# A transformer block in split fp32: w_out requested and cast later in the merge, another order of turns and operands at the entrance of the up stage, shorter norm steps

## The chip, the core and the metric

The kernel runs on one core of a Trainium2 chip. A core has TensorE (PE, matmuls), VectorE (DVE), ScalarE (ACT), GpSimd (POOL) and SyncE (SP), which here issues the DMAs; 16 DMA engines move data between HBM and SBUF. Each engine works through its own row of instructions in order, and semaphores hold an instruction back until what it reads is there. The metric is the time of one execution on the device in microseconds, as a median of runs.

## The reference

One layer of a hybrid block over 1024 tokens of width 1024, all in float32. Cut to the steps that matter here:

```python
attn = banded_window_attention(q, k, v, kc, vc, sink[l])
# merge_branches:
m = sigmoid(g_a) * (attn @ w_pa) + sigmoid(g_f) * (fourier_mix(f) @ w_pf)
y = m @ w_out
x = x + gt1 * rmsnorm(y, g_post1)
h2 = modulate(rmsnorm(x, g_pre2), sh2, sc2)      # h * (1 + scale) + shift
u, gate = split(h2 @ w_up)                       # ConvFFN, d_ff = 2816
u = u[:-2] * conv_w[0] + u[1:-1] * conv_w[1] + u[2:] * conv_w[2] + conv_b
x = x + gt2 * rmsnorm((silu(u) * gate) @ w_down, g_post2)
```

`rmsnorm(x, g)` is `x * rsqrt(mean(x*x) + eps) * g`.

## The kernel before

**Split products.** Every float32 operand of a large product is cast to a shorter type (the "hi" part, on ACT), and the rest, value minus hi, is the "lo" part (on VectorE, `sub`). `mm3` multiplies hi by hi, hi by lo and lo by hi: three matmuls of 128x128 by 128x512 for one step k. So nearly all of TensorE's operands come by an ACT cast and a VectorE subtraction. In the names, `h...` or `...h` is hi and `l...` or `...l` is lo.

**The program is one list.** Nothing is scheduled later: each engine's row has the order in which the Python code calls the steps. A step that is called earlier goes ahead on all engines that it uses.

**Merge.** Sixteen tiles `PA[i]` = (j, h): 128 channels j of m by 512 tokens h. `pa_mm` makes attn @ w_pa for one (12 matmuls, PSUM tile `pa`). `pa_out` multiplies it by the sigmoid gate (`sga`, read back from HBM), adds the Fourier half (`mf`, read back too) and casts `mh`; `pa_low` makes `ml`. `pa_load` requests `sga` and `mf` of the tile three ahead, into a ring of eleven buffers (`so`). `merge(i)` does the matmuls of tile i and then the sums of tile i-1. The first two tiles are made ahead of this loop (EARLY = 2). The w_pa tiles for j = 4 to 7 (`wpa`, parts `whpa` and `wlpa`) and the first half of w_out (`wor`, hi and lo parts in `w0a`, `w0b`) are loaded and cast inside the loop: `merge(i)` requests w_out's k = i - 2, casts it, and on even i does the same for a w_pa tile. w_out's second half (`woh`, `wol`) comes behind the loop.

**y = m @ w_out.** `y_mm(tk, h, ks)` adds steps k to a tile of 128 tokens tk by 512 columns h. `y_token` does the norm of y, the residual and the norm of x (`y_square`, `y_norm`, `y_gate`, `y_res`, `x_sq`, `z_scale`). `y_norm` takes the mean square v, a square root on ACT, a reciprocal r on VectorE, and one Newton step r (1.5 - 0.5 v r r). `y_turn` transposes z on TensorE (eight matmuls against the identity, `ptz`), and `y_affine` applies scale and shift (a2, s2) from PSUM in eight pieces, on VectorE (V) or ACT (None).

**Up stage.** h2 @ w_up in Winograd's form of Strassen's algorithm: the activations give the operands B11, B21, T1, T2, T3, T4n, B22 (`hb_puts` casts and subtracts four column tiles c; `t1` to `t4` are the sums ahead of it on `h`), the weights give P1, P2, P5, P6, P7 (`conv` makes hP on ACT, lP on VectorE). `mm(n)` is one product, accumulated in PSUM as `X_u`, `Y_u`, `Z_u`; `evac(n)` takes it out (`snP`, and `u` sums on VectorE); `ahead(n)` makes weight parts that come next. All three are called from a list written out by hand at the entrance, and from a table behind it.

Of the kernel before, what the change touches and what calls it, by code (L numbers as in the profile page):

```python
# [12 lines left out]
AF = mybir.ActivationFunctionType  # L13
# [22 lines left out]
def fbits(ap):  # L36
    return ap.bitcast(F)
# [26 lines left out]
def block_kernel(ctx: ExitStack, tc: tile.TileContext, t: dict, out: bass.AP, dbg: dict):  # L64
# [18 lines left out]
    def s(name, dtype=F):  # L83
        return spool.tile([P, 512], dtype, tag="s", name=name, bufs=40)
# [1369 lines left out]

    wo, w0s = {}, []

    def wo_load(k, h):
        raw = s(f"wor{k}{h}")
        load(out=raw, in_=t["w_out"][k * P:(k + 1) * P, h * 512:(h + 1) * 512])
        if h == 0:  # L1460
            if k == 0:
                w0 = [hbl.tile([P, 3, 512], R, tag="ha", name=f"w0a{i}", bufs=4) for i in range(4)]
                w0 = [w0[i][:, j, :] for i in range(4) for j in range(3)]
                w0s.extend(w0 + [hbl.tile([P, 1, 512], R, tag="hb", name=f"w0b{i}", bufs=4)[:, 0, :] for i in range(4)])
            wo[k, h] = (w0s[2 * k], w0s[2 * k + 1])
        else:
            wo[k, h] = (o2(f"woh{k}{h}", "w1", 16), o2(f"wol{k}{h}", "w1", 16))
        copy(wo[k, h][0], raw)
        return lambda: sub(wo[k, h][1], raw, fbits(wo[k, h][0]))

    def merge(i):

        j, h = PA[i]
        pa_mm(j, h, ps(f"pa{j}{h}"))
        if i + 3 < len(PA) and PA[i + 3] not in pal:
            pa_load(*PA[i + 3], so)
        low = []
        if i - EARLY < KT:
            low.append(wo_load(i - EARLY, 0))
        if i % 2 == 0 and 4 <= i // 2 + 2 < KT:  # L1480
            raw, m = merge_raw(t["w_pa"], i // 2 + 2, "pa"), i // 2 + 2
            paw[m] = s(f"whpa{m}", R), s(f"wlpa{m}", R)
            copy(paw[m][0], raw)
            low.append(lambda: sub(paw[m][1], raw, fbits(paw[m][0])))
        if i > EARLY:
            pa_out(*PA[i - 1])
        for f in low:
            f()
        if i > EARLY:
            pa_low(*PA[i - 1])  # L1490
# [26 lines left out]
    def y_norm(tk, n, fill=()):  # L1517

        fill = list(fill)

        def between():
            if fill:
                fill.pop(0)()

        ss = ssy[:, tk, 2 * n[0]:2 * n[0] + 2 * len(n)]
        v, sq, r, n1 = (tiny(f"{q}y{tk}{n[0]}", 2, 8)[:, :len(n)] for q in ("v", "sq", "r", "n1"))
        add(v, ss[:, 0::2], ss[:, 1::2])
        nc.vector.tensor_scalar(out=v, in0=v, scalar1=1.0 / D, scalar2=EPS, op0=ALU.mult, op1=ALU.add)
# [310 lines left out]
    with tc.manual_schedule():  # L1839
# [41 lines left out]
        for f in [wo_load(k, 1) for k in range(4, KT)]:
# [251 lines left out]
```

## Time and profile before

| | us |
|---|---|
| median of 3 runs (lowest, highest) | 1311.36 (1310.92, 1312.81) |
| the profiled execution, its own time | 1312.6 |
| its span in the profile | 1310.8 |
| busy in the span: TensorE, VectorE, ACT, GpSimd | 1260.3, 1034.5, 683.3, 231.5 |

The profiled execution is one more execution of the same program; its span is from its first to its last instruction. TensorE is busy for 96% of it, and is 73% of the chain of work that ended last, VectorE 15%. "Busy" counts the time in which an engine executes something, not the time in which it stands waiting. In a row of the trace, `[3.29 <-ACT whpa L1483]` says that the engine stood idle for 3.29 us ahead of this instruction, and that what released it was ACT's instruction on line 1483 that wrote `whpa`. `x4` on a row joins four like instructions that follow each other. The merge lies from about 515 to 563 us of the span, y from 563 to 658, and the up stage begins there.

### The profile page before, as it was taken

The numbers are of one execution on the slowest core, as the hardware profiler recorded it, in microseconds if no ns is written. First come the engines' busy times: TensorE is split into PE (matmuls) and PEld (weight loads), VectorE is DVE, ScalarE is ACT, GpSimd is POOL, SyncE is SP. The second block draws the span as 40 slices with busy tenths as digits, with TensorE's granted clock in tenths as the row PEclk, the third lists the DMA queues.
The fourth block names the chain that finished last, engine by engine and source line by source line (L and its number), as shares of the span: only waits on it lengthen the run. The fifth ranks groups of instructions, "written<-read, shape, count | busy, mean of one in ns | idle before, by whom it ended". The sixth has DMA issues, their size and how long they took to land.

```text
span 1310.8 us, 18510 instructions
## 1 busy us (share of the span) xinstructions
PE 1260.3 (96%) x5998; PEld 1022.7 (78%) x5998; DVE 1034.5 (79%) x1890; ACT 683.3 (52%) x1358; POOL 231.5 (18%) x191
## 2 busy tenths in 40 slices
PE   5999999999999999899999999999999999999996
PEld 3768777888878877778867888888888887888884
DVE  4866768884888996677879998999888877666767
ACT  7754347433667775344566655445444445544442
POOL 0001211100333333000000023535554200000000
PEclk9999999999999999999999999999999999999998
DMA  9997464605233444745213586777867669987884
GB/s 314 352 328 222 143 219 147 192 21 162 59 113 112 127 131 128 267 154 153 89 41 97 148 255 208 225 219 221 250 185 211 196 210 296 370 262 226 285 283 148
DMA packets 271573, 254.56 MB, mean 194 GB/s; under 512 B 16732, under 2 KB 206836, under 8 KB 271476
## 3 DMA queue, kind: packets, MB, share of 16 engines
q1 hardware_dynamic: 271476, 253.38, 61.8%
q8 instruction: 47, 0.77, 0.2%
q14 instruction: 50, 0.41, 0.1%
HBM read 179.65 MB, written 73.40 MB: 193 GB/s over the span
## 4 chain that ended last, share of the span: by engine, by line
PE 73%; DVE 15%; ACT 4%; DMA 3%; issue 3%; SPq 1%; POOL 1%; DVEq 0%; POOLq 0%; ACTq 0%
PE X_u L110 5%; PE X_u L108 5%; PE X_u L109 5%; PE X_d L110 3%; PE X_d L109 3%; PE X_d L108 3%; PE Y_u L108 3%; PE Y_u L110 3%; PE Y_u L109 3%; PE X_g L108 2%; PE X_g L110 2%; PE X_g L109 2%; DVE p L1199 2%; DVE pl L91 2%; PE Y_d L108 1%
## 5 line engine op out<-in xcount | busy, mean ns | idle before, releaser
L91 DVE TENSOR_TENSOR lP_u<-A_u,hP_u 128x512 fp32r<-128x512 f32 x132 | 106.9, 814 | 23.1 <-ACT hP_u L330 21.4
L392 ACT COPY snP_u<-X_u 128x512 f32<-128x512 f32 x57 | 33.4, 586 | 131.8 <-PE X_u L110 131.7
L392 ACT COPY snP_d<-X_d 128x512 f32<-128x512 f32 x48 | 28.2, 587 | 99.0 <-PE X_d L110 94.9
L330 ACT CAST hP_u<-A_u 128x512 fp32r<-128x512 f32 x121 | 74.6, 619 | 0.0
L1219 POOL TENSOR_SCALAR p<-p,sm 128x640 f32<-128x640 f32 (+1 forms) x64 | 48.3, 774 | 91.5 <-PE pp L1224 35.3
L103 ACT CAST ph<-pp 128x512 fp32r<-128x512 f32 x76 | 44.3, 584 | 22.2 <-PE pp L1224 20.9
L91 DVE TENSOR_TENSOR pl<-pp,ph 128x512 fp32r<-128x512 f32 x76 | 51.6, 681 | 2.5 <-ACT ph L103 2.0
L91 DVE TENSOR_TENSOR yd<-yd,snP_d 128x512 f32<-128x512 f32 x36 | 24.8, 690 | 34.4 <-ACT snP_d L392 34.4
L1213 ACT ACTIVATE p<-p,nm 128x640 f32<-128x640 f32 (+1 forms) x64 | 51.4, 802 | 0.7 <-DVE nm L1206 0.7
L1199 DVE CUSTOM_DVE_ANT_0 p<-ss,mask 128x640 f32<-128x640 f32 (+1 forms) x64 | 49.9, 780 | 0.0
L91 POOL TENSOR_TENSOR A_u<-A_u,A_u 128x512 f32<-128x512 f32 x28 | 47.4, 1692 | 13.9 <-DVE lP_u L91 6.9
L1224 PE MATMUL pp<-ident,p 128*128 128x128 f32 x304 | 46.6, 273 | 2.8 <-POOL p L1219 1.5
L1224 PEld LDWEIGHTS pp<-ident,p 128*128 128x128 f32 x304 | 37.2, 140 | 11.7 <-POOL p L1219 2.9
L1634 DVE SCALAR_TENSOR_TENSOR tb<-u,vec,tb 128x1024 f32<-128x1024 f32 x22 | 39.5, 1795 | 2.8 <-ACT tb L1631 2.7
L91 POOL TENSOR_TENSOR S_u<-A_u,A_u 128x512 f32<-128x512 f32 x14 | 24.7, 1763 | 88.6 <-DMA g_d0P<-ghP 81.7
L1195 PE MATMUL ss<-kst,qs 128*128 128x384 f32 (+1 forms) x128 | 36.6, 367 | 1.3 <-DVE mx L1199 0.8
L91 DVE TENSOR_TENSOR lP_g<-A_g,hP_g 128x512 fp32r<-128x512 f32 x48 | 33.3, 701 | 5.3 <-ACT hP_g L103 4.3
L91 POOL TENSOR_TENSOR A_u<-S_u,A_u 128x512 f32<-128x512 f32 x14 | 18.7, 1337 | 104.1 <-DVE lP_u L91 104.1
L91 DVE TENSOR_TENSOR wB<-wB,wB 128x512 f32<-128x512 f32 x44 | 37.1, 842 | 0.0
L1635 DVE SCALAR_TENSOR_TENSOR tb<-u,vec,tb 128x1024 f32<-128x1024 f32 x22 | 35.6, 1617 | 0.9
L1235 PE MATMUL po<-pl,vst 128*128 128x512 f32 x76 | 31.3, 411 | 2.6 <-DVE pl L91 2.0
L320 ACT COPY snP_g<-X_g 128x512 f32<-128x512 f32 x24 | 14.1, 588 | 36.4 <-PE X_g L110 35.6
(886 smaller groups left out, 4365.3 us busy)
## 6 DMA issues: line engine op xcount, KB each, us to landing
A_u<-in_w_up SPq DMA_DIRECT2D x88, 256.0 KB, 4.5
wB<-in_w_down SPq DMA_DIRECT2D x44, 256.0 KB, 4.3
wa<-in_w_mod SPq DMA_DIRECT2D x36, 256.0 KB, 5.3
wt_dT<-wB SPq DMA_DIRECT2D x33, 256.0 KB, 2.5
wdB<-in_w_down SPq DMA_DIRECT2D x33, 256.0 KB, 4.4
wdT<-wt_dT SPq DMA_DIRECT2D x33, 256.0 KB, 3.3
A_g<-in_w_in SPq DMA_DIRECT2D x32, 256.0 KB, 5.0
ws<-in_w_mod SPq DMA_DIRECT2D x30, 256.0 KB, 6.0
```

What stands on the lines that cost most here:

```text
L91: return (eng or nc.vector).tensor_tensor(out=out, in0=a, in1=b, op=op)
L103: copy(hi, src)
L108: nc.tensor.matmul(ps, ah, bh, start=start, stop=False, skip_group_check=True)
L109: nc.tensor.matmul(ps, ah, bl, start=False, stop=False, skip_group_check=True)
L110: nc.tensor.matmul(ps, al, bh, start=False, stop=stop, skip_group_check=True)
L330: copy(st[j]["half", p][0], st[j][STA[p]])
L392: copy(d["s" + p], d["X"])
L1199: nc.vector.tensor_tensor_reduce(out=p_, in0=ssc[:, lo:768], in1=self.mk, op0=ALU.add, op1=ALU.max, scale=1.0, scalar=-3.0e38, accum_out=s ...
L1213: nc.scalar.activation(out=self.pt[g], in_=self.pt[g], func=AF.Exp, scale=SCALE, bias=self.m[:, g:g + 1], accum_out=self.sm[:, g:g + 1])
L1219: nc.gpsimd.tensor_scalar(out=self.pt[g], in0=self.pt[g], scalar1=self.sm[:, g:g + 1], scalar2=1.0, op0=ALU.mult, op1=ALU.mult)
L1224: nc.tensor.transpose(pp[:, g * P:(g + 1) * P], self.pt[g][:, j * P:(j + 1) * P], ident)
L1634: nc.vector.scalar_tensor_tensor(out=tb, in0=u[:, 0:1024], scalar=cw[0], in1=tb, op0=ALU.mult, op1=ALU.add)
```

## The change

**Merge.** w_out's first half is requested three merges later (in merges 5 to 12) and cast two merges after its request (7 to 14). A w_pa tile is requested one pair of merges ahead of its cast, and the cast stands ahead of the other work of its merge. Two tiles of w_out's second half are requested in the last merge, two right behind the last sums, four ahead of the residual's loads; their casts stay behind the last sums.

**w_out stage.** Step k=0 of token 2 goes ahead of k = 6, 7 of tokens 0 and 1. For token 2 all eight steps of the second half stand ahead of the turn of token 1 (six before).

**Norm steps.** For one column, four VectorE operations become two: n1 = (r v) r and r = (n1 - 3) r. This r is -2 times that of before, so G1 (two tiles) and a2 are scaled by -0.5 on ACT, once. For two columns (once) four become three.

**Entrance of the up stage.** `mm(1)` runs whole ahead of the turn of token 6. `conv(1, "P5")` and the four T2 sums come sooner, and the last four affines of token 7 go from ACT to VectorE. `evac(11)` goes ahead of the operand B22.

```diff
+    def wo_raw(k, h):
+        wor[k, h] = s(f"wor{k}{h}")
+        load(out=wor[k, h], in_=t["w_out"][k * P:(k + 1) * P, h * 512:(h + 1) * 512])
...
+    for n_, q_ in enumerate([(k, 0) for k in range(KT)] + [(0, 1), (1, 1)]):
+        WO.setdefault(5 + n_ if n_ < 11 else len(PA) - 1, []).append(q_)
+        if q_[1] == 0:
+            WOS.setdefault(min(n_ + 7, len(PA) - 1), []).append(q_)
...
         pa_mm(j, h, ps(f"pa{j}{h}"))
-        if i + 3 < len(PA) and PA[i + 3] not in pal:
-            pa_load(*PA[i + 3], so)
         low = []
-        if i - EARLY < KT:
-            low.append(wo_load(i - EARLY, 0))
         if i % 2 == 0 and 4 <= i // 2 + 2 < KT:
-            raw, m = merge_raw(t["w_pa"], i // 2 + 2, "pa"), i // 2 + 2
+            m = i // 2 + 2
+            raw = wpr.pop(m)
             paw[m] = s(f"whpa{m}", R), s(f"wlpa{m}", R)
             copy(paw[m][0], raw)
             low.append(lambda: sub(paw[m][1], raw, fbits(paw[m][0])))
+        if i % 2 == 0 and 4 <= i // 2 + 3 < KT:
+            m1 = i // 2 + 3
+            wpr[m1] = merge_raw(t["w_pa"], m1, "pa")
+        if i + 3 < len(PA) and PA[i + 3] not in pal:
+            pa_load(*PA[i + 3], so)
+        for q in WO.get(i, ()):
+            wo_raw(*q)
+        for q in WOS.get(i, ()):
+            low.append(wo_load(*q))
...
+    for x in (*G1, a2):
+        nc.scalar.activation(out=x, in_=x, func=AF.Copy, scale=-0.5)
...
-        mul(n1, r, r)
-        mul(n1, n1, v)
-        nc.vector.tensor_scalar(out=n1, in0=n1, scalar1=-0.5, scalar2=1.5, op0=ALU.mult, op1=ALU.add)
-        mul(r, r, n1)
+        if len(n) == 1:
+            nc.vector.scalar_tensor_tensor(out=n1, in0=r, scalar=v, in1=r, op0=ALU.mult, op1=ALU.mult)
+        else:
+            mul(n1, r, r)
+            mul(n1, n1, v)
+        nc.vector.scalar_tensor_tensor(out=r, in0=n1, scalar=-3.0, in1=r, op0=ALU.add, op1=ALU.mult)
...
             y_mm(tk, 0, range(6))
+        y_mm(2, 0, range(1))
...
-            y_mm(tk, 1, range(6))
+            y_mm(tk, 1, range(KT if tk == 2 else 6))
             y_turn(tk - 1)
-            y_mm(tk, 1, range(6, KT))
+            if tk > 2:
+                y_mm(tk, 1, range(6, KT))
...
-        mm(1, range(2))
+        mm(1)
         y_turn(6)
-        mm(1, range(2, 4))
...
         conv(0, "P5")
+        conv(1, "P5")
+        t2(0)
+        t2(1)
         y_affine(6, range(4, 8), None)
-        y_affine(7, range(4, 8), None)
+        y_affine(7, range(4, 8), V)
+        t2(2)
+        t2(3)
         mm(4)
...
         evac(0)
-        conv(1, "P5")
         conv(2, "P5")
         mm(5)
-        for c in range(4):
-            t2(c)
         evac(1)
...
         hb_puts(hb, "T4n", {c: h2[c, 0] for c in range(4)})
+        ahead(11)
+        evac(11)
         hb_puts(hb, "B22", {c: h2[c + 4, 1] for c in range(4)})
-        for k in range(11, 14):
+        for k in range(12, 14):
```

Three places show how the rows move. First ACT at the start of the merge loop, from the last casts of attn (`ah`) on. Before:

```order
L103 CAST ah_5679<-aT_3229 128x512
L103 CAST ah_5683<-aT_3229 128x512
L1468 CAST w0a_5774<-wor_5772 128x512
L1468 CAST w0a_5774<-wor_5801 128x512
L1345 CAST mh_5806<-mf_5668 128x512
L1468 CAST w0a_5775<-wor_5828 128x512
L1483 CAST whpa_5833<-wpa_5831 128x512
L1345 CAST mh_5838<-mf_5672 128x512
L1468 CAST w0a_5776<-wor_5861 128x512
```

After:

```order
L103 CAST ah_5679<-aT_3229 128x512
L103 CAST ah_5683<-aT_3229 128x512
L1345 CAST mh_5796<-mf_5668 128x512
L1518 ACTIVATE G_5703<-G_5703 128x512
L1518 ACTIVATE G_5704<-G_5704 128x512
L1494 CAST whpa_5813<-wpa_5775 128x512
L1345 CAST mh_5824<-mf_5672 128x512
L1345 CAST mh_5850<-mf_5676 128x512
L1494 CAST whpa_5867<-wpa_5816 128x512
L1345 CAST mh_5880<-mf_5688 128x512
L1475 CAST w0a_5904<-wor_5846 128x512
```

The w_out casts (`w0a`) stood first and between the casts of m (`mh`); now three `mh` casts, the two G scales and two w_pa casts (`whpa`) stand ahead of the first of them.

Second, VectorE at the entrance of the up stage, from the first lo part of P5 (`lP_u<-S_u`) on; the rows `h<-h,h` are the T2 sums. Before:

```order
L91 TENSOR_TENSOR lP_u_7262<-S_u_6625,hP_u_7261 128x512
L91 TENSOR_TENSOR lP_u_7299<-S_u_6753,hP_u_7298 128x512
L91 TENSOR_TENSOR lP_u_7303<-S_u_6875,hP_u_7302 128x512
L91 TENSOR_TENSOR h_6402<-h_6820,h_6402 128x512
L91 TENSOR_TENSOR h_6449<-h_6952,h_6449 128x512
L91 TENSOR_TENSOR h_6569<-h_7165,h_6569 128x512
L91 TENSOR_TENSOR h_6697<-h_7221,h_6697 128x512
L91 TENSOR_TENSOR u_7290<-Z_u_7240,snP_u_7296 128x512
L91 TENSOR_TENSOR lP_u_7329<-A_u_6367,hP_u_7328 128x512
```

After:

```order
L91 TENSOR_TENSOR lP_u_7236<-S_u_6612,hP_u_7235 128x512
L91 TENSOR_TENSOR lP_u_7240<-S_u_6736,hP_u_7239 128x512
L91 TENSOR_TENSOR h_6397<-h_6803,h_6397 128x512
L91 TENSOR_TENSOR h_6450<-h_6931,h_6450 128x512
L1594 TENSOR_SCALAR h_7195<-ptz_7189,a_71,s_72 128x128 x4
L91 TENSOR_TENSOR h_6560<-h_7147,h_6560 128x512
L91 TENSOR_TENSOR h_6684<-h_7195,h_6684 128x512
L91 TENSOR_TENSOR lP_u_7281<-S_u_6854,hP_u_7280 128x512
L91 TENSOR_TENSOR u_7272<-Z_u_7214,snP_u_7278 128x512
```

Two T2 sums stand ahead of the third lo part now and two behind four affines that ACT had.

Third, ACT from the last T4n cast on, where `hP_u` and `snP_u` behind the B22 casts belong to `ahead(11)` and `evac(11)`. Before:

```order
L103 CAST T4nb_7099<-h_6697 128x128
L103 CAST B22a_7101<-h_6820 128x3x128
L103 CAST B22a_7101<-h_6952 128x3x128
L103 CAST B22a_7101<-h_7165 128x3x128
L103 CAST B22a_7101<-h_7221 128x3x128
L103 CAST B22b_7103<-h_6820 128x128
L103 CAST B22b_7103<-h_6952 128x128
L103 CAST B22b_7103<-h_7165 128x128
L103 CAST B22b_7103<-h_7221 128x128
L330 CAST hP_u_7543<-A_u_6891 128x512
L320 COPY snP_u_7546<-X_u_7109 128x512
L330 CAST hP_u_7551<-A_u_6511 128x512
```

After:

```order
L103 CAST T4nb_7076<-h_6684 128x128
L330 CAST hP_u_7501<-A_u_6870 128x512
L320 COPY snP_u_7504<-X_u_7086 128x512
L103 CAST B22a_7078<-h_6803 128x3x128
L103 CAST B22a_7078<-h_6931 128x3x128
L103 CAST B22a_7078<-h_7147 128x3x128
L103 CAST B22a_7078<-h_7195 128x3x128
L103 CAST B22b_7080<-h_6803 128x128
L103 CAST B22b_7080<-h_6931 128x128
L103 CAST B22b_7080<-h_7147 128x128
L103 CAST B22b_7080<-h_7195 128x128
L330 CAST hP_u_7525<-A_u_6502 128x512
```

One `hP_u` cast and one `snP_u` copy have moved ahead of the eight B22 casts; the lo part of that cast moves the same way on VectorE.

## Rows read from the trace of the kernel before

**Rows 1.** Stage table: window, busy us per engine (instructions), granted clock, DMA share, GB/s.

```profile
521.00:546.00 25.00, 25.00 (x111) 20.57 (x110) 16.03 (x25) 7.87 (x13) 0.00 (x0) 1.00 0.84 299
546.00:554.00 8.00, 4.71 (x14) 3.42 (x13) 4.77 (x8) 2.89 (x5) 0.00 (x0) 0.79 0.68 203
...
690.00:720.00 30.00, 28.63 (x125) 23.12 (x124) 29.65 (x59) 21.35 (x47) 0.00 (x0) 1.00 0.37 106
```

**Rows 2.** TensorE, merge and w_out: start, duration, engine, line, operation, tiles, idle before.

```profile
546.02 0.39 PE L110 MATMUL pa<-ah,wlpa 128*128 128x512 f32 x1
549.69 0.79 PE L108 MATMUL pa<-ah,whpa 128*128 128x512 f32 x1 [3.29 <-ACT whpa L1483]
...
562.78 0.39 PE L110 MATMUL pa<-ah,wlpa 128*128 128x512 f32 x1
...
586.05 0.39 PE L108 MATMUL y<-w0a,mh 128*128 128x512 f32 x1
```

**Rows 3.** TensorE at the turn of token 1.

```profile
597.65 0.88 PE L185 MATMUL ptz<-ident,z 128*128 128x128 f32 x6 [1.03 <-DVE z L1556]
```

**Rows 4.** TensorE at the entrance of the up stage.

```profile
663.25 0.55 PE L185 MATMUL ptz<-ident,z 128*128 128x128 f32 x3 [1.01 <-ACT z L1554]
...
678.83 0.50 PE L108 MATMUL Y_u<-T1a,hP_u 128*128 128x512 f32 x1 [0.51 <-ACT hP_u L103]
...
686.24 0.50 PE L109 MATMUL X_u<-T2a,hP_u 128*128 128x512 f32 x1 [1.17 <-DVE T2a L91]
...
703.57 0.50 PE L108 MATMUL X_u<-T4na,hP_u 128*128 128x512 f32 x1 [0.94 <-ACT snP_u L320]
...
704.73 0.50 PE L110 MATMUL X_u<-T4na,lP_u 128*128 128x512 f32 x1 [0.43 <-DVE lP_u L91]
```

**Rows 5.** SyncE in the merge: DMA issues.

```profile
523.03 0.33 SPq L1459 DMA_DIRECT2D wor<-in_w_out  x1
...
535.37 0.32 SPq L1329 DMA_DIRECT2D sga<-sga_d  x1
543.00 0.32 SPq L1329 DMA_DIRECT2D mf<-mf_d  x1
```

**Rows 6.** ACT in the merge.

```profile
528.39 0.62 ACT L1468 CAST w0a<-wor 128x512 fp32r<-128x512 f32 x1 [8.79 <-DMA wor<-in_w_out]
...
549.02 0.62 ACT L1483 CAST whpa<-wpa 128x512 fp32r<-128x512 f32 x1 [0.27 <-DMA wpa<-in_w_pa]
```

**Rows 7.** VectorE in the merge: first multiply of four tiles.

```profile
532.59 0.68 DVE L91 TENSOR_TENSOR sga<-pa,sga 128x512 f32<-128x512 f32 x1
...
535.73 0.68 DVE L91 TENSOR_TENSOR sga<-pa,sga 128x512 f32<-128x512 f32 x1
...
558.31 0.68 DVE L91 TENSOR_TENSOR sga<-pa,sga 128x512 f32<-128x512 f32 x1
...
561.01 0.68 DVE L91 TENSOR_TENSOR sga<-pa,sga 128x512 f32<-128x512 f32 x1
```

**Rows 8.** VectorE, two steps of a norm.

```profile
583.30 0.16 DVE L91 TENSOR_TENSOR n1y<-ry 128x1 f32<-128x1 f32 x1
583.50 0.16 DVE L91 TENSOR_TENSOR n1y<-n1y,vy 128x1 f32<-128x1 f32 x1
```

**Rows 9.** Groups by line and form, VectorE: count, busy us, mean ns.

```profile
L173 DVE SCALAR_TENSOR_TENSOR n1d<-rd,vd 128x1 f32<-128x1 f32 x8 | 1.8, 220 | 0.3
```

**Rows 10.** ACT at the entrance of the up stage.

```profile
674.89 2.89 ACT L1568 ACTIVATE h<-ptz,s,a 128x128 f32<-128x128 f32 x8
...
699.96 1.75 ACT L103 CAST B22a<-h 128x384 fp32r<-128x384 f32 x4
```

**Rows 11.** VectorE: four affines of turn 0, then the entrance.

```profile
597.91 1.36 DVE L1570 TENSOR_SCALAR h<-ptz,a,s 128x128 f32<-128x128 f32 x4
...
678.81 1.29 DVE L91 TENSOR_TENSOR lP_u<-S_u,hP_u 128x512 fp32r<-128x512 f32 x2 [3.10 <-ACT hP_u L103]
...
703.99 0.69 DVE L91 TENSOR_TENSOR lP_u<-A_u,hP_u 128x512 fp32r<-128x512 f32 x1
```

More of the change, by code (lines that the diff above doesn't have):

```diff
@@ L1455, in block_kernel @@
     wo, w0s = {}, []
+    wor = {}
+    def wo_raw(k, h):
+        wor[k, h] = s(f"wor{k}{h}")
+        load(out=wor[k, h], in_=t["w_out"][k * P:(k + 1) * P, h * 512:(h + 1) * 512])
     def wo_load(k, h):
-        raw = s(f"wor{k}{h}")
-        load(out=raw, in_=t["w_out"][k * P:(k + 1) * P, h * 512:(h + 1) * 512])
+        if (k, h) not in wor:
+            wo_raw(k, h)
+        raw = wor[k, h]
         if h == 0:
@@ L1469, in wo_load @@
         return lambda: sub(wo[k, h][1], raw, fbits(wo[k, h][0]))
+    wpr = {}
+    WO, WOS = {}, {}
+    for n_, q_ in enumerate([(k, 0) for k in range(KT)] + [(0, 1), (1, 1)]):
+        WO.setdefault(5 + n_ if n_ < 11 else len(PA) - 1, []).append(q_)
+        if q_[1] == 0:
+            WOS.setdefault(min(n_ + 7, len(PA) - 1), []).append(q_)
     def merge(i):
@@ L1871, in block_kernel @@
         pa_out(*PA[-1])
+        wo_raw(2, 1)
+        wo_raw(3, 1)
+        pa_low(*PA[-1])
         low = [wo_load(k, 1) for k in range(4)]
-        for f in (lambda: pa_low(*PA[-1]), *low):
+        for f in low:
             f()
+        for k in range(4, KT):
+            wo_raw(k, 1)
         xr_load(0)
@@ L1894, in block_kernel @@
                 pre(tk - 2, ("A22",))
-            y_mm(tk, 0, range(6))
+            y_mm(tk, 0, range(1 if tk == 2 else 0, 6))
             if tk == 2:
```

## The prediction

> **What bounds the kernel now.** The change touches three stretches: the merge, the w_out stage behind it, and the entrance of the up stage. I read the stage table first, to see whether TensorE is held there, and then TensorE's own rows. From 521 to 546 it is busy 25.00 us of 25 with 111 matmuls, 0.227 us for one, and 12 x 0.227 = 2.72 for a tile of the merge [rows 1]. So a change can win only what TensorE loses standing. Then it stands 3.29 us for a cast of w_pa, and the granted clock falls from 1.00 (the upper level, 2.4 GHz) to a mean of 0.79 from 546 to 554 [rows 1, 2], so part of that stretch is at the lower level of 1.2. From 546.02 to 562.78 lie 48 matmuls, worth 48 x 0.227 = 10.9; they took 16.76. **Lost: 5.9.** The next 96, up to 586.05, took 23.27 for 21.8, from 562.78 on [rows 2]. **Lost: 1.4.** A turn of token 1 waits 1.03 for z [rows 3]. TensorE's rows from 658 to 705 hold five waits: 1.01, 0.51, 1.17, 0.94, 0.43 [rows 4]. **Together 4.1.** All of this sums to 12.4, and each piece is at a place that the change reorders.
>
> **Why the merge is late.** The first w_out tile is requested at 523.03 [rows 5]; its cast begins at 528.39, after ACT has idled for 8.79 [rows 6]: a request takes 5.4 us to land, with the DMA engines 0.84 busy [rows 1]. The cast stands in the merge that requests it, ahead of the casts of m on ACT. VectorE waits with it, and then needs 2.70 us for a tile (558.31 to 561.01) and 3.14 (532.59 to 535.73) where two weight parts fall into it [rows 7]. That is TensorE's own pace, so it never catches up. Its late sums hold the ring of eleven buffers: SyncE issues nothing between 535.37 and 543.00 [rows 5]. The w_pa tile requested behind comes late, and the cast that TensorE waits for begins at 549.02 [rows 6].
>
> **The merge after the change.** The w_pa tile for j=4 takes the place of that first w_out request, so it lands at 523.0 + 5.4 = 528.4. G is requested ahead of it. No row shows a scale of 128x512 in place on ACT; the cast of this shape takes 0.62 [rows 6], and I take that for each of two. With both behind 528.4 at the worst, the cast of w_pa ends at 530.3 and its low part (0.68, as each VectorE step of this shape in [rows 7]) at 530.9. TensorE, not held, starts the tile that reads it at 546.25 - 4 x 2.72 = 535.4: 4.5 us to spare. VectorE by then has the tiles summed that TensorE finished before 525, and goes on from 530.9 with twelve at 2.70 and twice 0.44 more: 530.9 + 32.4 + 0.9 = 564.2. TensorE ends the merge at 546.25 + 4 x 2.72 = 557.1. It then has k 0 to 5 of tokens 0 and 1 and the one step of token 2 that was pulled forward, 13 x 0.68 = 8.8, before it needs k=6 of m at 566; VectorE is past those at about 561. The woh casts follow ACT's last m cast, the first low part of woh can end at 565.4, and TensorE wants it at 557.1 + 17 x 0.68 = 568.7. Both losses go: **-7.3**. With a cycle of 3.0 instead of 2.70 the first low part would be at 569.0, and 0.3 would stay.
>
> **Norm steps.** Four VectorE operations, 0.20 from start to start [rows 8], become two scalar_tensor_tensor. On 128x1 with a pointer as scalar one takes 0.22 elsewhere in this kernel [rows 9]; the one with a constant I put between 0.16 (the small multiply [rows 8]) and 0.22. With 0.04 between them the pair takes 0.44 to 0.5 against 0.8: about 0.3 saved in each of 14 norms, 4.2 us of VectorE, nearly all under TensorE. If the pair took as long as the four, only 0.6 at the turn of token 1 would be lost again. The scales that it needs (two of 128x512, one of 128x8) are some 1.4 us of ACT in idle time, the 8.79 above.
>
> **The turn of token 1.** It waited 1.03 [rows 3]. Both norms of the token are 0.3 shorter, and one k more stands between the token's last matmul and the turn (two moved in front of the turn, one moved out to the start): 0.6 + 0.68 = 1.28. The wait goes with 0.25 to spare: **-1.0**. Turn 0 loses 0.68 of cover and gains 0.6; I allow 0 to 0.2 there, and as much at turn 2.
>
> **The up entrance.** With mm(1) whole ahead of it, turn 6 comes 12 x 0.227 = 2.72 later, and its z was 1.01 late: that wait goes. conv(1, "P5") stood behind eight ACT affines of 2.89 [rows 10]; four now go behind it and four to VectorE, and the 0.51 on hP_u goes. VectorE, idle for 3.10 there [rows 11], starts the T2 sums in that gap. Four affines cost it 1.36 [rows 11], three norms give 0.9 back, so T2's low parts come 3.1 - 0.5 = 2.6 sooner, and TensorE wants them 1.0 + 0.5 sooner: 1.17 + 1.5 - 2.6 leaves 0.1 of that wait. The last two (0.94 on snP_u, 0.43 on lP_u) came behind ACT's casts of B22, the first four of them 1.75 [rows 10], and behind B22's low parts on VectorE, which end where lP_u begins, at 703.99 [rows 11]; hP, snP and lP of evac(11) now come ahead of them. All together **-4.0**, and 0.1 for each of four or five restarts, whose first matmuls take 0.50 instead of 0.39 [rows 2, 4]: **-0.4**.
>
> What comes back: from 690 to 720 VectorE is busy 29.65 of 30 [rows 1]. TensorE gains 4.4 there, VectorE only the 2.6, so what VectorE delivers comes up to 1.8 nearer to its use. What was less ahead becomes a wait; B22's own parts are later by evac(11), about 0.7. I keep 0 to 1.8 and take **+0.3**, near the lower end, as the waits of before come from where things stand in a row and not from VectorE's total.
>
> **A rule that speaks against the change.** At 528.39 a cast of ACT waits for its transfer, and what stands behind it in ACT's row waits too, for 8.79 us [rows 6]. So the G scales ahead of the w_pa cast hand on whatever G is late. Rival 2 prices that from rows. The Trainium skill has it as a rule (TensorE: Matmul & The Clock Gate, "Engine queue depths": ScalarE and VectorE have queues that are strictly first in, first out). The trace agrees with that rule by the same 8.79.
>
> **The sum.** Against the profiled execution of 1312.6 (span 1310.8): -7.3 - 1.0 - 4.0 - 0.4 + 0.3 = -12.4, so 1300.2. The median of the runs, 1311.4, lies 1.2 below that execution: 1311.4 - 12.4 = **1299.0**.
>
> **Rivals.**
> 1. *The entrance gives its gain back.* VectorE is the bound from 690 on, and TensorE only waits elsewhere: 1.8 to 4 of the 4.4 return. For it: 29.65 of 30 busy [rows 1]. Against it: the waits that go were ones of order, three of the five on ACT [rows 4]. Time: 1299.0 + 1.5 to 3.7 = 1300.5 to 1302.7. Chance 0.25.
> 2. *ACT's row hands on a late transfer.* G or w_pa lands later than 5.4 after its request, ACT stands, and the chain on VectorE ends later than 564.2. The slack is 4.5 at the first tile and 3.3 at the start of woh; a wait of 3 to 5 needs a landing of 11 or more. For it: the 8.79 of before [rows 6]; against it: the request itself took 5.4 [rows 5, 6]. Time 1302 to 1304. Chance 0.10.
> 3. *The change does nothing:* VectorE's twelve tiles end the merge, not TensorE. To return 7.3 its chain must end at 575, which takes a cycle of 3.6; the rows have 2.70 and 3.14 [rows 7]. With rival 1 beside it: 1309 to 1313. Chance 0.04.
> 4. *Slower.* A w_out request waits for buffers that VectorE frees, VectorE for a cast, and the cast for the request before. In my walk a turn of that loop is 2.7, and k=7 is requested near 550, lands at 555.4 and is read at 566.6. Were each turn to pay a landing, it would be 2.7 + 5.4 = 8.1. Eight turns use up the 10 us of slack and then the 12.4 of gain from (10 + 12.4) / 8 = 2.8 more a turn, 5.5 in all; at 6.0 the time is 1311.4 + 8 x 0.5 = 1315. For it: the gap at SyncE [rows 5]; against it: requests now run two merges ahead of their casts. Chance 0.03.
>
> **How the numbers follow.** The forecast has 0.58, the rivals 0.25, 0.10, 0.04 and 0.03. The forecast alone spans 1297.8 (nothing comes back, 0.3, and each restart costs 0.2 to 0.3 and not 0.1, 0.9 more) to 1300.5 (all of the 1.8 comes back). Up to 1304 it takes in the first two rivals; down to 1296.3 the 1.5 by which single runs of before lie apart from their median. Under 2 in 10 is left out. About 0.2% (2.6 us) is what a measurement of this kernel can tell from no change; the forecast and rivals 1 and 2 all lie beyond it. Faster 0.93, same 0.04, slower 0.03.
>
> **What would show it.** Right: between 515 and 590 no wait of TensorE over 0.5, the clock at 1.00 all through the merge, the first w_out matmul near 557 instead of 563; no wait at turns 1 and 6, none on snP_u behind T4n. Wrong: a gap of several us at SyncE in the merge; ACT idle on G; TensorE waiting on VectorE for 1 us or more at T3, T4n or B22, or new waits on VectorE from 720 to 800 that sum to over 1.8.

## The result and the profile after

The changed kernel takes 1300.34 us (median of 5 runs, 1299.59 to 1301.67), the kernel before 1312.59 (5 runs, 1310.92 to 1312.97). The ratio is 0.9909, with a 95% interval of 0.9897 to 0.9922: 12.2 us less, where 12.4 less were forecast. The profiled execution took 1300.34, with a span of 1298.6.

The stage table of the changed kernel, with the columns of [rows 1]:

```profile
521.00:546.00 25.00, 24.90 (x110) 20.60 (x111) 18.80 (x31) 9.79 (x17) 0.00 (x0) 1.00 1.04 347
546.00:554.00 8.00, 8.00 (x37) 6.63 (x36) 7.76 (x13) 3.43 (x6) 0.00 (x0) 1.00 0.86 271
...
680.00:710.00 30.00, 29.87 (x132) 24.43 (x131) 29.65 (x59) 21.76 (x48) 0.00 (x0) 1.00 0.37 105
```

From 546 to 554 TensorE now works throughout, at a granted clock of 1.00 (4.71 of 8 and 0.79 in [rows 1]). The last row is about the stretch that was 690 to 720 before: VectorE is as full as it was, 29.65 of 30, and TensorE works 29.87 instead of 28.63.

To see where the time went I use TensorE's rows that open each stretch: the last wait on attn ahead of the merge, the first w_out matmul, the first turn, the first matmul with B11, T1, T4n and B22, and the first of the down stage. In the changed kernel they are:

```profile
521.10 0.50 PE L109 MATMUL pa<-al,whpa 128*128 128x512 f32 x1 [0.78 <-DVE al L91]
...
557.75 0.39 PE L108 MATMUL y<-w0a,mh 128*128 128x512 f32 x1
...
583.59 1.03 PE L185 MATMUL ptz<-ident,z 128*128 128x128 f32 x8
...
650.21 0.39 PE L108 MATMUL X_u<-B11a,hP_u 128*128 128x512 f32 x1
...
666.42 0.50 PE L108 MATMUL Y_u<-T1a,hP_u 128*128 128x512 f32 x1
...
691.93 0.39 PE L108 MATMUL X_u<-T4na,hP_u 128*128 128x512 f32 x1
694.65 0.39 PE L108 MATMUL Y_u<-B22a,hP_u 128*128 128x512 f32 x1
...
1069.39 0.39 PE L108 MATMUL X_d<-dB,bP_d 128*128 128x512 f32 x1
```

The differences of these starts, worked out in the same way for every kernel that ran (us; the last two columns are the median time and its count of runs):

| kernel | merge | w_out to turn 0 | to B11 | to T1 | to T4n | to B22 | to down stage | median | runs |
|---|---|---|---|---|---|---|---|---|---|
| before | 42.59 | 27.14 | 67.85 | 17.05 | 28.53 | 3.55 | 374.47 | 1312.59 | 5 |
| changed | 36.65 | 25.84 | 66.62 | 16.21 | 25.51 | 2.72 | 374.74 | 1300.34 | 5 |
| e1 merge alone | 36.61 | 25.84 | 67.84 | 17.05 | 28.52 | 3.57 | 374.50 | 1305.59 | 5 |
| e2 norms alone | 41.71 | 27.20 | 66.58 | 16.28 | 28.47 | 3.56 | 374.33 | 1309.41 | 7 |
| e3 entrance alone | 42.80 | 27.23 | 67.82 | 17.04 | 25.53 | 2.71 | 374.76 | 1308.80 | 7 |
| e5 no short norms | 36.67 | 26.31 | 67.07 | 17.03 | 25.54 | 2.72 | 374.64 | 1302.32 | 5 |
| e6 request in the same merge | 36.66 | 30.12 | 66.62 | 16.20 | 25.53 | 2.72 | 374.78 | 1302.03 | 4 |
| e7 w_pa alone | 39.31 | 27.34 | 67.85 | 17.34 | 28.52 | 3.57 | 374.30 | 1309.91 | 10 |
| e8 lo parts twice | 38.23 | 28.55 | 66.59 | 16.49 | 25.52 | 2.72 | 374.85 | 1305.30 | 4 |
| e9 evac(11) back | 36.62 | 25.84 | 66.56 | 16.21 | 26.62 | 3.58 | 374.31 | 1301.24 | 5 |
| e10 T2 and P5 back | 36.63 | 25.85 | 66.55 | 16.21 | 27.46 | 2.73 | 374.65 | 1301.74 | 4 |
| e11 two more waits | 36.62 | 25.85 | 66.62 | 15.97 | 24.92 | 2.72 | 375.38 | 1299.55 | 4 |
| e12 old order of w_out | 36.61 | 25.85 | 66.62 | 16.20 | 25.52 | 2.72 | 374.73 | 1300.04 | 4 |
| e13 scales alone | 41.56 | 27.24 | 67.87 | 17.07 | 28.53 | 3.57 | 374.44 | 1312.70 | 11 |

From before to changed the columns give -5.94, -1.30, -1.23, -0.84, -3.02, -0.83 and +0.27, together -12.89. The stretch ahead of the first column ended 0.69 later in the changed kernel's execution (521.10 against 520.41), and behind the last nothing moved (the last matmul starts 218.67 later in both): -12.20, the difference of the two spans. Outside the merge a stretch that a kernel does not touch repeats to 0.1 us or so (0.3 at worst, the stretch to T1 in e7 and e8), while the start of the program, which no kernel here changes, ended anywhere from 519.5 to 524.4. So small effects are read from this table and not from medians.

The rows that answer to [rows 5 to 7]. SyncE in the merge:

```profile
523.12 0.38 SPq L1249 DMA_DIRECT2D wpa<-in_w_pa  x1
...
529.46 0.33 SPq L1461 DMA_DIRECT2D wor<-in_w_out  x1
...
535.86 0.33 SPq L1329 DMA_DIRECT2D sga<-sga_d  x1
538.14 0.33 SPq L1329 DMA_DIRECT2D mf<-mf_d  x1
```

ACT:

```profile
527.83 1.30 ACT L1518 ACTIVATE G<-G 128x512 f32<-128x512 f32 x2 [3.13 <-DMA G<-gt_d]
529.42 0.62 ACT L1494 CAST whpa<-wpa 128x512 fp32r<-128x512 f32 x1 [0.29 <-DMA wpa<-in_w_pa]
...
535.96 0.61 ACT L1475 CAST w0a<-wor 128x512 fp32r<-128x512 f32 x1
```

VectorE, the first lo part of w_pa, the last lo part of m, and a norm:

```profile
530.07 0.69 DVE L91 TENSOR_TENSOR wlpa<-wpa,whpa 128x512 fp32r<-128x512 f32 x1 [3.33 <-ACT whpa L1494]
...
564.02 0.69 DVE L91 TENSOR_TENSOR ml<-mf,mh 128x512 fp32r<-128x512 f32 x1 [0.69 <-ACT mh L1345]
...
577.44 0.22 DVE L1555 SCALAR_TENSOR_TENSOR n1y<-ry,vy 128x1 f32<-128x1 f32 x1
577.70 0.16 DVE L1559 SCALAR_TENSOR_TENSOR ry<-n1y,ry 128x1 f32<-128x1 f32 x1
577.89 0.75 DVE L1568 SCALAR_TENSOR_TENSOR z<-y,ry,G 128x512 f32<-128x512 f32 x1
```

SyncE's longest gap is now 2.3 us (535.86 to 538.14) instead of 7.6. The first w_out tile lies ready before its cast: requested at 529.46, cast at 535.96, with no wait on a transfer. (The first two tiles of w_out's second half are requested in merges 13 and 14, one in each, and not both in the last.) ACT and VectorE do stand for G and w_pa, 3.13 and 3.33 us, as the walk of the prediction had it, and TensorE does not notice.

TensorE at the entrance has two waits left of the five of [rows 4]; the first of them is new:

```profile
659.82 1.09 PE L185 MATMUL ptz<-ident,z 128*128 128x128 f32 x8 [0.39 <-DVE z L1580]
...
675.71 0.50 PE L109 MATMUL X_u<-T2a,hP_u 128*128 128x512 f32 x1 [0.33 <-DVE T2a L91]
```

### The profile page after: what moved, and what is told of

Read it like the earlier page. It is cut to its first block, busy times and chain, and to the rows that moved or that the text cites. A ratio compares the mean times of both kernels' runs of the same rounds, so it can differ in the third digit from the quotient of the medians.

```text
span 1298.6 us, 18497 instructions
## 1 busy us (share of the span) xinstructions
PE 1256.2 (97%) x5998; PEld 1022.1 (79%) x5998; DVE 1030.4 (79%) x1865; ACT 682.7 (53%) x1357; POOL 232.0 (18%) x191
## 4 chain that ended last, share of the span: by engine, by line
PE 79%; DVE 13%; ACT 3%; issue 2%; DMA 1%; POOL 1%; SPq 0%; DVEq 0%; POOLq 0%; ACTq 0%
PE X_u L110 5%; PE X_u L109 5%; PE X_u L108 5%; PE X_d L110 3%; PE X_d L109 3%; PE X_d L108 3%; PE Y_u L110 3%; PE Y_u L108 3%; PE Y_u L109 3%; PE X_g L108 2%; PE X_g L109 2%; PE X_g L110 2%; DVE p L1199 2%; DVE pl L91 2%; PE y L110 2%
```

## The experiments

**e1, the merge alone.** The kernel before with the merge hunks of the diff and nothing else:

```diff
...
+        for q in WO.get(i, ()):
+            wo_raw(*q)
+        for q in WOS.get(i, ()):
+            low.append(wo_load(*q))
...
```

> The kernel before with the new merge alone (order of turns, norm steps and entrance as before). Theory of the prediction: the 5.9 and 1.4 us lost around the w_pa cast and the start of woh go and nothing else does: 1312.6 - 7.3 = 1305.3 us, ratio 0.9944; the turn of token 1 still waits 1.0 and the entrance keeps its five waits, 4.1 together. Rival (the parts need each other, what the merge wins is waited for again at turn 1 or at the entrance): 1308 to 1312, and these waits grow.

Measured: 1305.59 us, ratio 0.9943 (0.9929 to 0.9956). Merge and w_out are the changed kernel's to 0.04, every stretch behind them is that of before to 0.03. The merge's gain stands by itself and is kept to the end.

**e2, the norm steps alone,** with the three scales on ACT:

```diff
-        mul(n1, r, r)
-        mul(n1, n1, v)
-        nc.vector.tensor_scalar(out=n1, in0=n1, scalar1=-0.5, scalar2=1.5, op0=ALU.mult, op1=ALU.add)
-        mul(r, r, n1)
+        if len(n) == 1:
+            nc.vector.scalar_tensor_tensor(out=n1, in0=r, scalar=v, in1=r, op0=ALU.mult, op1=ALU.mult)
...
+        nc.vector.scalar_tensor_tensor(out=r, in0=n1, scalar=-3.0, in1=r, op0=ALU.add, op1=ALU.mult)
```

> The kernel before with the shorter norm steps alone, the scaling of G1 and a2 among them. Theory: nearly all of the 4.2 us that VectorE saves lie under TensorE. Turn 1 waits 0.4 instead of 1.03, turn 6 0.8 instead of 1.0: -0.8. The G scales stand ahead of the first w_out cast on ACT, which then starts 0.7 later, at 529.1, and the old merge hands that on to TensorE: +0.7. Sum: 1312.5 (1311.5 to 1313.3). Rival A (VectorE's time is on the path): 1308.4. Rival B (a late row on ACT costs nothing): 1311.8, and the w_pa wait of 3.29 stays as it was.

Measured: 1309.41 us, ratio 0.9972 (0.9961 to 0.9983). Every expectation missed: -3.1 and not -0.1. The turn of token 1 does not wait at all:

```profile
594.96 0.39 PE L110 MATMUL y<-woh,ml 128*128 128x512 f32 x1
595.19 1.03 PE L185 MATMUL ptz<-ident,z 128*128 128x128 f32 x8
```

The stretch to B11 has the whole gain of the changed kernel (66.58), without the new order of w_out. Four short norms lie in one chain there, not two: VectorE works in order, and both norms of token 0 stand ahead of those of token 1. The chain runs from the reciprocal (`ry`) of token 0's first norm to token 1's z. Before, with TensorE's last matmul ahead of the turn:

```profile
583.11 0.16 DVE L1531 RECIPROCAL ry<-sqy 128x1 f32<-128x1 f32 x1 [1.17 <-ACT sqy L1529]
...
597.11 0.88 DVE L1556 TENSOR_SCALAR z<-xr,ry 128x512 f32<-128x512 f32 x2
```

```profile
596.24 0.39 PE L110 MATMUL y<-woh,ml 128*128 128x512 f32 x1
```

In e2, where that matmul is the one at 594.96 above:

```profile
581.80 0.16 DVE L1533 RECIPROCAL ry<-sqy 128x1 f32<-128x1 f32 x1 [1.17 <-ACT sqy L1531]
...
594.52 0.88 DVE L1560 TENSOR_SCALAR z<-xr,ry 128x512 f32<-128x512 f32 x2
```

Counted from that matmul the reciprocal stands where it stood (13.1 to 13.2 us ahead), and z starts 0.44 ahead of it instead of 0.87 behind: 1.31 sooner, 0.33 for each of the four. The wait and its restart had cost 1.27; three norms would not have covered it. The other -0.8 is at turn 6 (16.28). The merge was 0.9 shorter, and the scales did not delay it; e13 asks why.

**e3, the entrance alone:**

```diff
-        mm(1, range(2))
+        mm(1)
         y_turn(6)
-        mm(1, range(2, 4))
...
+        conv(1, "P5")
+        t2(0)
...
+        ahead(11)
+        evac(11)
...
```

> The kernel before with the new entrance of the up stage alone. Theory: the waits of 1.01 (turn 6), 0.51 (hP), 0.94 (snP) and 0.43 (lP) go; with the long norm steps T2 comes 0.9 later than in the full change, so about 1 us of T2a's 1.17 stays: 1312.6 - 3.4 = 1309.2, ratio 0.9974. Rival (VectorE is the bound from 690 on and gives the gain back): 1310.5 to 1312.5, with new waits on VectorE between 690 and 800.

Measured: 1308.80 us, ratio 0.9970 (0.9958 to 0.9982). The sum came as expected, its place did not. T4n and B22 have the full gain (25.53, 2.71), T2a waits 0.33 as in the full change, and the stretch to T1 gains nothing (17.04), because turn 7 waits where turn 6 did:

```profile
667.82 1.09 PE L185 MATMUL ptz<-ident,z 128*128 128x128 f32 x8 [1.15 <-DVE z L1556]
```

**e5, the whole change with the four norm steps of before** (and G1, a2 not scaled):

```diff
...
-        nc.vector.scalar_tensor_tensor(out=r, in0=n1, scalar=-3.0, in1=r, op0=ALU.add, op1=ALU.mult)
+        mul(n1, r, r)
+        mul(n1, n1, v)
+        nc.vector.tensor_scalar(out=n1, in0=n1, scalar1=-0.5, scalar2=1.5, op0=ALU.mult, op1=ALU.add)
+        mul(r, r, n1)
```

> The whole change without the shorter norm steps. Theory: turn 1 waits 1.03 - 0.68 = 0.35 again, turn 0 about 0.4, turn 7 0.7 instead of 0.39 and T2a 0.9 instead of 0.33: 1300.3 + 1.6 = 1301.9. Rival A (norm steps hidden everywhere, worth nothing): 1300.3. Rival B (all of VectorE's 4.2 us are on the path): 1304.5.

Measured: 1302.32 us, ratio 0.9913 to before (0.9897 to 0.9929). The stretches against the changed kernel: turn 0 +0.47, to B11 +0.45, to T1 +0.82, to T4n +0.03. That sums to 1.8, where 1.6 was expected. T2a did not take part; turn 7 (a wait of 1.15) took its share. So what the short norms save on VectorE (14 times 0.33, some 4.6 us) is worth 1.8 here and 2.0 in e2 (1.27 and 0.77): what lies on the chains to z at two or three turns, and next to nothing elsewhere.

**e6, requests in the merge that casts:**

```diff
-        WO.setdefault(5 + n_ if n_ < 11 else len(PA) - 1, []).append(q_)
+        if q_[1] == 1:
+            WO.setdefault(5 + n_ if n_ < 11 else len(PA) - 1, []).append(q_)
```

> The whole change, but each tile of w_out's first half is requested in the merge that casts it (7 to 14), not two merges earlier. It separates the earlier w_pa and the later casts from the distance of two merges. Theory: a request waits for the ring, which VectorE frees, then 4 to 5.4 us for landing, and the m cast of that merge stands behind it: two tiles take about 6.5 instead of 5.4, eight merges end 4 to 5 later, and the slack takes most of it: 1300.3 + 1 (0 to 3) = 1301.3, ACT idle on w_out transfers for several us in all. Rival A (the distance is the whole gain of the merge): 1307. Rival B (the distance does nothing): 1300.3, no idle time of ACT on w_out.

Measured: 1302.03 us, ratio 0.9925 to before (0.9908 to 0.9941). ACT stands for w_out tiles again, 16.4 us in six waits; the longest one, and the wait that reaches TensorE:

```profile
549.48 0.62 ACT L1475 CAST w0a<-wor 128x512 fp32r<-128x512 f32 x1 [5.16 <-DMA wor<-in_w_out]
```

```profile
570.38 0.50 PE L108 MATMUL y<-w0b,mh 128*128 128x512 f32 x1 [1.70 <-ACT mh L1345]
```

In the profiled execution the stretch to turn 0 is 4.3 longer: 1.7 is this wait, and in the rest TensorE runs at the lower level behind it (granted clock 0.50 from 572 to 575) and meets the first tiles of w_out's second half just as they are made. So the distance of two merges is what keeps ACT from standing. Its lack is not felt in the merge itself, which stays at 36.66, but at the end of the chain, where the slack is used up. The median (+1.7) is within what was expected; its four runs lie 5.9 apart (1299.93 to 1305.88). The trace is of the slowest of them, and the fastest is as fast as the changed kernel, so what the distance is worth differs from run to run. That this hangs on when each tile lands is likely, but one trace does not show it.

**e7, w_pa alone** requested a pair of merges earlier and cast first, w_out as before:

```diff
...
+            raw = wpr.pop(m)
             paw[m] = s(f"whpa{m}", R), s(f"wlpa{m}", R)
             copy(paw[m][0], raw)
...
+            wpr[m1] = merge_raw(t["w_pa"], m1, "pa")
...
```

> The kernel before with the w_pa tiles alone requested one pair of merges earlier and cast ahead of the rest; w_out as before (requested and cast in merges 2 to 9). Theory: the wait of 3.29 on the w_pa cast goes, but VectorE still starts its sums 8 us late behind the first w_out cast, so the last sums of m come near 570 and TensorE waits some 4 us at the start of w_out instead: 1312.5 - 3 = 1309.5 (1308 to 1311). Rival (w_pa's place is the whole cause): 1305.5 to 1306.5, no wait at the start of w_out.

Measured: 1309.91 us, ratio 0.9984 (0.9975 to 0.9993). The time is the expected one. ACT's first w_out cast is as late as before, and TensorE's wait is now for a lo part of w_pa:

```profile
529.22 0.62 ACT L1468 CAST w0a<-wor 128x512 fp32r<-128x512 f32 x1 [9.96 <-DMA wor<-in_w_out]
```

```profile
554.25 0.50 PE L110 MATMUL pa<-ah,wlpa 128*128 128x512 f32 x1 [1.29 <-DVE wlpa L91]
...
571.05 0.50 PE L108 MATMUL y<-woh,mh 128*128 128x512 f32 x1 [0.60 <-ACT woh L1468]
```

I had put the 4 us that stay at the start of w_out; 2.7 of them stayed in the merge (39.31 against 36.65) and 1.5 behind it (27.34 against 25.84). The cause is the one named: VectorE's late chain, which w_pa's place does not touch. Its last lo part of m begins at 570.51, where the changed kernel has 564.02.

**e8, the lo parts of m computed twice** from j=2 on (the same values, so only VectorE's work grows):

```diff
-        sub(msp[j, h][1], pal[j, h][1], fbits(msp[j, h][0]))
+        for _ in range(2 if j >= 2 else 1):
+            sub(msp[j, h][1], pal[j, h][1], fbits(msp[j, h][0]))
```

> The whole change, with the lo part of each m tile from j=2 on computed twice (the same values again): 12 VectorE operations more, 0.6 each, 7.3 us in all. Theory: VectorE's chain is hidden with some 4 us of slack, so a cycle of 3.3 instead of 2.7 costs TensorE only what is over it: waits of about 4 us at k=7 of w_out and at woh, 1300.3 + 4 = 1304.3 (2.5 to 5). Rival A (VectorE's chain already ends the merge): +7.3, 1307.6. Rival B (far more slack): +0 to 1.

Measured: 1305.30 us, ratio 0.9946 to before (0.9933 to 0.9960), 5.0 over the changed kernel. In the profiled execution the stretch to turn 0 is 2.7 longer, and the merge 1.6, the latter from the clock (last section) and not from VectorE: no row of the merge waits. TensorE's waits are at woh:

```profile
571.48 0.50 PE L108 MATMUL y<-woh,mh 128*128 128x512 f32 x1 [0.59 <-ACT woh L1476]
573.01 0.50 PE L109 MATMUL y<-wol,mh 128*128 128x512 f32 x1 [1.04 <-DVE wol L91]
```

The slack follows from the first lo part of w_out's second half (`wol`). In the changed kernel it is ready at 564.63 + 0.69 = 565.3, and TensorE reads it 4.2 later:

```profile
564.63 4.90 DVE L91 TENSOR_TENSOR wol<-wor,woh 128x512 fp32r<-128x512 f32 x8
```

```profile
569.53 0.39 PE L109 MATMUL y<-wol,mh 128*128 128x512 f32 x1
```

In e8 it begins at

```profile
572.27 4.90 DVE L91 TENSOR_TENSOR wol<-wor,woh 128x512 fp32r<-128x512 f32 x8
```

Counted from the first w_out matmul (558.65 in e8, 557.75 in the changed kernel) that is 6.7 later, and TensorE reads it 2.6 later: 6.7 - 2.6 = 4.1, the same slack, where the prediction had 3.3. Rival 3 would have cost the whole 6.7.

**e9, evac(11) behind B22 again:**

```diff
-        ahead(11)
-        evac(11)
         hb_puts(hb, "B22", {c: h2[c + 4, 1] for c in range(4)})
-        for k in range(12, 14):
+        for k in range(11, 14):
```

> The whole change, but ahead(11) and evac(11) behind the operand B22 again. Theory: the waits of 0.94 on snP and 0.43 on lP come back with their restarts: 1300.3 + 1.5 = 1301.8. Rival (VectorE's total is the bound there, B22 comes 0.7 sooner and pays it back): 1300.3 to 1300.8, and the waits that come back are matched by others that go.

Measured: 1301.24 us, 0.9 over the changed kernel, which the spread of the runs does not separate from it; the stretches do. To T4n +1.11, to B22 +0.86, to the down stage -0.43: +1.5 net. Both waits are back:

```profile
692.40 0.50 PE L108 MATMUL X_u<-T4na,hP_u 128*128 128x512 f32 x1 [0.92 <-ACT snP_u L320]
...
693.56 0.50 PE L110 MATMUL X_u<-T4na,lP_u 128*128 128x512 f32 x1 [0.43 <-DVE lP_u L91]
```

**e10, T2 and P5 back:**

```diff
-        conv(1, "P5")
-        t2(0)
-        t2(1)
         y_affine(6, range(4, 8), None)
-        y_affine(7, range(4, 8), V)
-        t2(2)
-        t2(3)
+        y_affine(7, range(4, 8), None)
...
+        conv(1, "P5")
         conv(2, "P5")
         mm(5)
+        for c in range(4):
+            t2(c)
```

> The whole change, but conv(1, P5), the four T2 sums and the last affines of token 7 (on ACT) where they were before. Theory: the wait on hP (0.5) comes back, and T2a's wait of 0.33 grows to 1.2 or more, since TensorE comes to it sooner than before: the stretch from T1 to T4n takes 1.5 to 2.0 longer than its 25.51, 1300.3 + 1.8 = 1302.1. Rival (VectorE's total is the bound, so the order of T2 and P5 does not matter): the stretch or the one behind it gives all but 0.5 back, 1300.8.

Measured: 1301.74 us, 1.4 over the changed kernel. The stretch to T4n takes 1.95 longer, and what comes back later (0.1) is no more than that stretch varies between kernels that do not touch it. TensorE's waits:

```profile
670.10 0.50 PE L108 MATMUL Y_u<-T1a,hP_u 128*128 128x512 f32 x1 [0.50 <-ACT hP_u L103]
...
677.51 0.50 PE L109 MATMUL X_u<-T2a,hP_u 128*128 128x512 f32 x1 [1.16 <-DVE T2a L91]
```

**e11, two steps beyond the change:**

```diff
-        y_norm(8, (1,), [lambda: t1(1)])
+        y_norm(8, (1,))
...
         z_scale(7, 0, V)
+        t1(1)
         mm(2)
...
-        evac(4)
         hb_puts(hb, "T2", {c: h2[c, 0] for c in range(4)})
+        evac(4)
```

> The whole change and two steps more: t1(1) behind z_scale of token 7, not in the middle of its norm, and evac(4) behind the operand T2. They aim at the two waits that are left at the entrance, 0.39 for z at turn 7 and 0.33 for T2a's lo part. Theory: turn 7's wait shrinks by 0.3 and T2a's goes, 1300.3 - 0.7 = 1299.6 with the two stretches 0.3 shorter each; a difference that the time alone can hardly show. Rival (the second sum or the evacuation is then late itself): the stretches stay at 16.2 and 25.5 or grow.

Measured: 1299.55 us (1298.91 to 1301.80), lower than the changed kernel by less than the runs of either lie apart. To T1 -0.24, to T4n -0.59, as aimed at; to the down stage +0.64. A new wait of 0.73 stands right behind:

```profile
694.08 0.50 PE L110 MATMUL Y_u<-B22a,lP_u 128*128 128x512 f32 x1 [0.73 <-DVE lP_u L91]
```

Net -0.2. VectorE has no idle time there from 663 to this lo part, so its total has become the bound, and the mechanism of the prediction's rival 1 is seen at work.

**e12, the old order of w_out** in the changed kernel:

```diff
-        y_mm(2, 0, range(1))
...
-            y_mm(tk, 0, range(1 if tk == 2 else 0, 6))
+            y_mm(tk, 0, range(6))
...
-            y_mm(tk, 1, range(KT if tk == 2 else 6))
+            y_mm(tk, 1, range(6))
             y_turn(tk - 1)
-            if tk > 2:
-                y_mm(tk, 1, range(6, KT))
+            y_mm(tk, 1, range(6, KT))
```

> The whole change without the new order of the w_out stage (step k=0 of token 2 pulled forward, all eight steps of its second half ahead of turn 1). Theory, revised after the run with the norm steps alone, where the wait at turn 1 went without any of this: three norms stand in the row ahead of turn 1's z, not two, 1.0 together, so the order is worth nothing beside the short norms: 1300.3 (within 0.3), the stretch from turn 0 to the up stage stays at 66.6. Rival (the prediction's own sum, 0.6 from the norms and 0.68 from the order): a wait of 0.4 at turn 1 comes back, 1300.8.

Measured: 1300.04 us, and no stretch differs from the changed kernel by more than 0.04. Beside the short norms this part of the change does nothing. (By the rows of e2 the norms ahead of this z are four, not the three of the expectation.)

**e13, the scales on ACT alone,** by 1.0, in the kernel before:

```diff
+    for x in (*G1, a2):
+        nc.scalar.activation(out=x, in_=x, func=AF.Copy, scale=1.0)
```

> The kernel before with the ACT instructions on G1 and a2 alone, scaling by 1.0, with nothing else changed. It asks whether the 0.9 us by which the merge was shorter in the run with the norm steps came from ACT's G scales standing ahead of the first w_out cast, or from when transfers landed in that execution. Theory: the landing; the stretch from the last wait on attn to the first w_out matmul is again 42.6 to 42.8 and the time 1312.5 (within 1). Rival A (the scales shorten the merge): 41.7 and 1311.5. Rival B (the prediction's rule, they delay it): over 43.2.

Measured: 1312.70 us (11 runs), ratio 0.9997 (0.9989 to 1.0006): the scales cost nothing. But the merge took 41.56 in the profiled execution, as in e2, so the number that I had given for "the landing" was wrong. It was wrong because e3's 42.80, my yardstick, holds 1.6 us of lower clock at its start (last section); without them it is 41.2, and e3 has no scales. The old merge takes 41.2 to 42.6 in four profiled executions. They differ in how long TensorE waits for the cast of w_pa: 2.17 to 2.40 in e2, e3 and e13, and 3.29 in the profiled execution of before, which was at the upper end. Rival A falls with e3's corrected number and with the time. One thing stays open: e2's median lies 3.1 below that of before, while its stretches behind the merge give 2.2, and the scales give none of the rest.

## Why the prediction was right, and where it was not

**The merge and the start of w_out** (-7.3 forecast, -5.94 - 1.30 = -7.24 between the two profiled executions, -6.9 in e1's median). The walk holds row by row, to 0.5 us: lo part of w_pa ending at 530.8 (530.9 forecast), the last lo part of m at 564.7 (564.2), the first w_out matmul at 557.75, which is 557.1 after taking off the 0.69 by which this execution came later to the merge. The 1.4 at the start of w_out has one matmul too few (97 rows start from 562.78 to 586.05, not 96), so 1.2 were lost there. e7 shows that w_pa's place alone gives 2.5 of the median (1312.38 - 1309.91), e6 that ACT stands again if the requests do not run ahead of the casts, e8 how much slack is left. Against the old merge of e2, e3 and e13 (41.2 to 41.7) the two stretches gain 6.0 to 6.4, against that of the kernel before 7.2, and the interval of e1's time takes in both (5.8 to 9.3).

**The turn of token 1** (-1.0 forecast, -1.23). The size was right by luck, since its working was not. The step that failed is "Both norms of the token are 0.3 shorter, and one k more": four norms count, which bring z 1.3 sooner by themselves, and the k more gives nothing beside them (e2, e12). Without the short norms the order does help turn 1 by 0.8 but costs turn 0 0.47 (e5).

**The entrance** (-4.4 forecast, -0.84 - 3.02 - 0.83 = -4.69). Two sizes in it were off, in opposite directions, and that they nearly cancel is luck. "With mm(1) whole ahead of it ... that wait goes" left out that turn 7 comes next on the same chain: 0.39 is waited there, and 1.15 without the short norms, so moving mm(1) is worth nothing by itself (e3). Beside the short norms it is worth 0.07 (16.28 in e2, 16.21 in the changed kernel): the gain to T1 is nearly all theirs. On the other side a restart cost more than the 0.1 that I took. To T4n and B22 the waits that went sum to 0.51 + 0.84 + 0.94 + 0.43 = 2.72, and the stretches lost 3.85. Read from start to start of the matmuls, each of the three waits that went whole (hP_u, snP_u, lP_u) had cost 0.25 to 0.29 more than its idle time; T2a's restart stays, and the rest is nearly all one more stop of 0.27 just behind hP_u, which the trace shows without idle time. T2a kept 0.33 where 0.1 was forecast.

**What came back** (+0.3 forecast, +0.27): the stretch to the down stage. It answers to rival 1, which asked for 1.8 to 4. The waits of before were indeed of order: undone one by one (e9, e10) they return, and at most 0.4 of them is paid back behind. The bound is close, though: of e11's 0.83 VectorE took 0.64 back.

**Rival 2 and the rule on ACT's row.** ACT did stand for G, 3.13 us, with the w_pa cast behind it; the two landed 6.0 and 6.3 us after their requests and not 5.4, and the slack took it. So "ACT idle on G", named as a sign of being wrong, came true and cost nothing. The sign "between 515 and 590 no wait of TensorE over 0.5" was drawn too wide: it takes in three waits of 0.70 to 0.78 from 517 to 521, which the change does not touch. The other signs of being right held, and no other one of being wrong came. e6 shows the price when the slack does not suffice: 16.4 us of ACT's waits, 4.3 of TensorE's time in the traced execution. The Trainium skill's rule that ScalarE's queue is strictly first in, first out (TensorE: Matmul & The Clock Gate, "Engine queue depths") agrees with both rows; whether it costs anything is decided by the slack behind, which the rule does not speak of.

**The median.** 1299.0 was forecast from a median of 1311.36 in three runs; thirteen and fifteen runs of the same kernel later had 1312.4 to 1312.6. The difference was right to 0.2, the level by 1.3 off.

## What to carry to other kernels

A cast that waits for its transfer blocks its engine's whole row, so request a tile as many steps ahead as the landing takes, and read the price from what stands behind the cast, not from the cast. When a wait is removed, name the next one on the same chain, and count every instruction that stands ahead in the row, those of the neighbour's work too. Effects under a few us are read from stretches between fixed rows of the trace, which mostly repeat to 0.1 us here, and not from times that spread by 2 or more.

## What the hardware showed that I had not expected

Behind the same short waits TensorE's clock fell in one execution and not in the next. Every kernel here has three waits of 0.69 to 0.78 ahead of the merge. The stage rows of 518 to 530 are, in this order, of the changed kernel, e3 and e8:

```profile
518.00:530.00 12.00, 10.51 (x45) 8.12 (x44) 6.94 (x12) 4.19 (x9) 0.00 (x0) 1.00 0.98 318
```

```profile
518.00:530.00 12.00, 10.97 (x40) 8.67 (x41) 4.01 (x7) 1.72 (x4) 0.00 (x0) 0.86 1.01 348
```

```profile
518.00:530.00 12.00, 10.51 (x38) 7.98 (x37) 7.39 (x12) 4.17 (x7) 0.00 (x0) 0.86 1.01 316
```

In e8 the rows behind the last of these waits run 0.43 apart instead of 0.227, at the lower level of 1.2 GHz:

```profile
521.60 0.63 PE L110 MATMUL pa<-ah,wlpa 128*128 128x512 f32 x1
522.02 0.63 PE L108 MATMUL pa<-ah,whpa 128*128 128x512 f32 x1
522.45 0.63 PE L109 MATMUL pa<-al,whpa 128*128 128x512 f32 x1
```

Eight matmuls at 0.43 instead of 0.227 cost 1.6 us, twice what the longest of the waits took. So a wait that is taken away also takes away a chance of this, and a single profiled execution can be 1.6 us off for a reason that has nothing to do with the edit. Behind longer waits it fell in every execution that has them at this place: the w_pa waits of 2.17 to 3.29 of the old merge (before, e2, e3, e13; granted clock 0.79 to 0.83 from 546 to 554). Why one execution falls and another does not, these runs do not show.
